# A two-layer decoder on one core: transposing the residual stream's strips on VectorE and through memory instead of on TensorE

## The chip, the cores and the metric

The kernel runs on one core of a Trainium2 chip, as one launch. The metric is device time in microseconds (us): 2370.67 us is the median of three runs (2370.56 to 2370.95). A profile shows one execution; PE is TensorE (PEld its weight loads), DVE is VectorE, ACT is ScalarE, POOL is GpSimd, SP is SyncE, and a "q" behind a name is that engine's queue of DMA issues.

## What is computed

A decoder of two layers on 256 positions with 2048 features. The first layer has stick-breaking attention, the second a dilated sliding-window attention over keys and values made once; each is followed by a gated feed-forward part with a causal convolution and by a gate on a projected per-layer input. Cut to what matters:

```python
for i in range(DEPTH):                      # DEPTH = 2
    h = rms_norm(x, attn_norm_w[i])
    if i < N_A_LAYERS:
        x = x + mixer_a(h, a_w_qkv[i], a_w_o[i])
    else:
        if i == N_A_LAYERS:
            k_blocks, v_blocks = shared_kv_blocks(x, kv_norm_w, b_w_kv, positions)
        j = i - N_A_LAYERS
        x = x + mixer_b(h, b_w_q[j], b_w_o[j], k_blocks, v_blocks, positions)
    x = x + conv_ffn(rms_norm(x, ffn_norm_w[i]), ffn_w_up[i], ffn_conv_w[i], ffn_conv_b[i], ffn_w_down[i])
    gate = jax.nn.sigmoid(rms_norm(x, ple_norm_w[i]) @ ple_w_gate[i])
    x = x + gate * (p[i].astype(x.dtype) @ ple_w_proj[i])
return rms_norm(x, final_norm_w)
```

All inputs, weights and the output are float32. The feed-forward width is 5632.

## The kernel before

**Precision.** Each float32 operand of a large product is cut in two parts, a high one of the type `F32R` and the rest, and a product is made of three matmuls: high by high, high by low, low by high. Activations are cut by `split_x` (L135 to L145; ACT writes the high part at L140, VectorE the low part at L141, and both scale by the norm's gain) or `split` (L147). Weights come from memory in tiles `raw` of four k-blocks (a k-block is 128 rows by 512 columns; 4 buffers, issued by SP at L258) and are cut in pairs of k-blocks: ACT writes `whi` (L275), VectorE `wlo` (L276), each with 4 buffers (`NWSP`).

**The stream.** The residual `x` lies in two tiles `x[0]`, `x[1]` of 128 positions by 2048 features, and is worked on in four strips of 512 features (`strip_of`). The products that read it need it the other way round, features in the partitions: `h[4*s+o]` is feature block `o` of strip `s`, 128 features by 256 positions, high part on the left and low part on the right of a 128x512 tile.

**The products.** `strip_v` (L308) makes 128 positions by 512 outputs for both halves of the positions: per k-block and half three matmuls of 512 columns (L317, L318, L319). `strip_t` (L293) makes the transposed product: four output blocks of 128, per k-block and block one matmul of 512 columns (L302) and one of 256 (L305). Both take the k-blocks in pairs, in rising order, and keep the last pair of k-blocks for the end of each output.

**The stages.** `add_strips` (L557) multiplies with `wo_a`, `wdn` or `wo_b` strip by strip, adds into `x` (L565), squares it for the norm (L212) and, where a norm follows, turns the strip: `turn` (L237) makes eight TensorE transposes of 128x128 (L244) against an identity `idf` into two PSUM banks `two`, and `split_x` reads these. `ple` (L636) does the same after the gate (L656, L659, L660), and in the first layer copies the turned strip to `xT` too (L672), for keys and values. The stage that follows reads `h` in rising order, so it can begin while the last strip is being turned. `ffn` (L573) makes the gated inputs `g` in two parts of the 11 groups of four blocks, 6 and 5 (`half`, L604), with a product with `wdn` behind each, the first of them without a norm and without turns.

**Order.** The framework's planner lays out the order of each engine's instructions ahead of time: it goes by the program's order, with pieces such as the cutting of weights moved ahead (`high_priority`, L273), and by when it expects operands and buffers by its own costs. On the chip each engine then keeps that order and waits for semaphores. Tiles named `kb` come from one ring of `NRING` = 42 buffers of 128x512 (L67, L95): `h`, `g`, `qk`, `v`, `xT` and others share them. POOL issues nothing in this kernel and SP issues the weights.

Of the kernel before, what the change touches and what calls it, by code (L numbers as in the profile page):

```python
# [10 lines left out]
F32 = mybir.dt.float32  # L11
# [3 lines left out]
AF = mybir.ActivationFunctionType  # L15
OP = mybir.AluOpType

P = 128
S = 256
# [7 lines left out]
FB = FF // P  # L27
# [36 lines left out]

RAW = 4
WARM = 9
NRING, NRAW, NWSP = 42, 4, 4  # L67
AHEAD = 200
KV_AT = (0, 6, 12, 16)
PI_PARTS = _two_pi_parts()  # L70
# [3 lines left out]
def tile_trunk(ctx, tc, head_d, xT_d, x_d, pT_d, pos_d, vec_d, cst_d, csb_d, wqkv, wo_a, wkv, wq_b, wo_b, wup, wdn, wpg, wpp, gfin_d, out_d):  # L74
    nc = tc.nc
# [2 lines left out]
    wraw = ctx.enter_context(tc.tile_pool(name="wraw", bufs=NRAW))  # L78
    wsp = ctx.enter_context(tc.tile_pool(name="wsp", bufs=NWSP))
    tmp = ctx.enter_context(tc.tile_pool(name="tmp", bufs=3))  # L80
    psum = ctx.enter_context(tc.tile_pool(name="psum", bufs=8, space=bass.MemoryType.PSUM))

    uid = [0]

    def nm(s):
        uid[0] += 1
        return f"{s}_{uid[0]}"
# [4 lines left out]
    def two_banks():  # L92
        return psum.tile([P, 2, 512], F32, tag="two", bufs=1, name=nm("two"))

    def rt(s, shape=(P, 512), dt=F32):  # L95
        return ring.tile(list(shape), dt, tag="kb", name=nm(s))

    def tt(s, shape=(P, S), dt=F32, tag=None, bufs=None):
        kw = {} if bufs is None else {"bufs": bufs}
        return tmp.tile(list(shape), dt, tag=tag or s, name=nm(s), **kw)  # L100

    f32 = lambda ap: ap.bitcast(F32)
# [3 lines left out]
    x = [cst.tile([P, D], F32, name=f"x{t}") for t in range(2)]  # L106
# [22 lines left out]
    def gain(base, j):  # L129
        return vec[:, base + j : base + j + 1]  # L130


    last = {}

    def split_x(src, j, bases):  # L135

        out = []
        for b in bases:
            h = rt("h", dt=F32R)
            last["split"] = nc.scalar.activation(h[:, :S], src, AF.Copy, scale=gain(b, j)).ins  # L140
            nc.vector.scalar_tensor_tensor(  # L141
                h[:, S:], src, gain(b, j), f32(h[:, :S]), op0=OP.mult, op1=OP.subtract
            )
            out.append(h)
        return out  # L145

# [4 lines left out]
    def strip_of(t, s):  # L151
        return x[t][:, s * 512 : (s + 1) * 512]
# [83 lines left out]

    def turn(s):  # L237

        two = two_banks()
        out = [two[:, o // 2, (o % 2) * S : (o % 2 + 1) * S] for o in range(4)]  # L240
        for o, d in enumerate(out):
            for t in (1, 0):
                c = s * 512 + o * P
                nc.tensor.transpose(d[:, t * P : (t + 1) * P], x[t][:, c : c + P], idf)  # L244
        return two, out

    def weights(W, s, n, fine=False, before=lambda k0: None, block=None, base=0, ringed=0):

# [59 lines left out]
    def strip_v(W, s, xs, base=0, tail=2, ringed=0):  # L308

        n = len(xs)  # L310
        ps = [None] * 2
        for k, t, hi, lo in (g for group in steps(weights(W, s, n, base=base, ringed=ringed), n, 2, tail) for g in group):
            if k == 0:
                ps[t] = bank("accv", "acc")
            xh = xs[k][:, t * P : (t + 1) * P]
            xl = xs[k][:, S + t * P : S + (t + 1) * P]
            nc.tensor.matmul(ps[t], xl, hi, start=k == 0, stop=False)  # L317
            nc.tensor.matmul(ps[t], xh, lo, start=False, stop=False)  # L318
            nc.tensor.matmul(ps[t], xh, hi, start=False, stop=k == n - 1)  # L319
        return ps  # L320
# [236 lines left out]
    def add_strips(W, xs, gain_of, norm, base=0):  # L557

        out = []
        for s in range(4):  # L560
            ps = strip_v(W, s, xs, base)
            if norm is not None and s == 3:
                norm.table = load_table()
            for t in range(2):
                nc.vector.tensor_tensor(strip_of(t, s), ps[t], strip_of(t, s), op=OP.add)  # L565
                if norm is not None:
                    norm.add(s, t)
            if norm is not None:
                for o, b in enumerate(turn(s)[1]):
                    out += split_x(b, 4 * s + o, [gain_of])  # L570
        return out

    def ffn(i, xs, rstd):  # L573
        cv = V_CONV + i * 4 * 2 * FB

        def conv(j, ps, y):
            col = lambda r: vec[:, cv + r * 2 * FB + j : cv + r * 2 * FB + j + 1]
            u = tt("u", tag="t", bufs=6)
            evac(ps, rstd, u)
            nc.scalar.activation(y, u, AF.Identity, scale=col(2), bias=col(3))  # L580
            nc.vector.scalar_tensor_tensor(y[:, 1:], u[:, : S - 1], col(1), y[:, 1:], op0=OP.mult, op1=OP.add)
            nc.vector.scalar_tensor_tensor(y[:, 2:], u[:, : S - 2], col(0), y[:, 2:], op0=OP.mult, op1=OP.add)

        def part(strips):
            gs = []
            for s in strips:
                ps = strip_t(wup[i], s, xs)
                gates = []
                for o in range(4):
                    y = tt("gate", bufs=4)  # L590
                    conv(4 * s + o, ps[o], y)
                    silu = nc.scalar.activation(y, y, AF.Silu).ins
                    gates.append(y)
                ps = strip_t(wup[i], FB // 4 + s, xs)
                for o in range(4):
                    y = tt("val", tag="t", bufs=6)
                    conv(FB + 4 * s + o, ps[o], y)
                    nc.vector.tensor_tensor(y, y, gates[o], op=OP.mult)
                    g = rt("g", dt=F32R)
                    split(y, g)  # L600
                    gs.append(g)
            return gs, silu

        half = (FB // 4 + 1) // 2  # L604
        gs, _ = part(range(half))
        add_strips(wdn[i], gs, None, None)
        gs, silu = part(range(half, FB // 4))
        if i == 0:
            rotary_tables(silu)
        norm = Norm()  # L610
        h = add_strips(wdn[i], gs, G_PLE + i * KB, norm, base=4 * half)
        return h, norm

# [22 lines left out]
    def ple(i, xs, ps_, rc, norm, gain_of=None):  # L636

        out, raw, gf = [], [], []
        if gain_of is None:
            for s in range(4):  # L640
                t = rt("gfin")
                nc.scalar.dma_start(
                    t, bass.AP(tensor=gfin_d.tensor, offset=gfin_d.offset + 512 * s, ap=[[0, P], [1, 512]])
                )
                gf.append(t)
        for s in range(4):
            end = gain_of is None and s == 3
            if end:
                pr = strip_v(wpp[i], s, ps_)
                gp = strip_v(wpg[i], s, xs, tail=KB, ringed=KB // 2)  # L650
            else:
                gp = strip_v(wpg[i], s, xs)
                pr = strip_v(wpp[i], s, ps_)
            for t in range(2):
                g = tt("pg", (P, 768), tag="w", bufs=2)[:, :512]
                nc.scalar.activation(g, gp[t], AF.Sigmoid, scale=rc[:, t : t + 1])  # L656
                if s == 3 and (end or t == 1):
                    norm.table = load_table()
                nc.vector.tensor_tensor(g, pr[t], g, op=OP.mult)  # L659
                nc.vector.tensor_tensor(strip_of(t, s), strip_of(t, s), g, op=OP.add)  # L660
                norm.add(s, t)
                if end:
                    finish(t, norm.half(t), gf[3])
                elif gain_of is None:
                    nc.vector.tensor_tensor(strip_of(t, s), strip_of(t, s), gf[s], op=OP.mult)
                if end and t == 0:
                    tc.keep_in_program_order(nc.scalar.preload_act_table_set("sigmoid_and_others"))
            if gain_of is not None:
                two, bs = turn(s)
                for o in range(0, 4, 2):  # L670
                    r = rt("xT")
                    nc.scalar.activation(r, two[:, o // 2], AF.Copy)  # L672
                    raw += [r[:, :S], r[:, S:]]
                    for q in range(2):
                        out += split_x(bs[o + q], 4 * s + o + q, [gain_of])
        return out, raw


    idf = cst.tile([P, P], F32, name="idf")
    warm_up()  # L680
    norm = FirstNorm()
    h = [None] * KB
# [33 lines left out]
    o = mixer_a(h, rstd, rc, first)  # L716
    for i in range(2):
        norm = Norm()
        h = add_strips(wo_a if i == 0 else wo_b, o, G_FFN + i * KB, norm)
        rstd, _ = norm.done()  # L720
        pb = p_blocks(i)
        h, norm = ffn(i, h, rstd)
        _, rc = norm.done(row=False)
        norm = Norm()
        if i == 0:
            hq, xT = ple(i, h, pb, rc, norm, G_ATTN + KB)
            rstd, rc = norm.done()
            o = mixer_b(hq, lambda js: [split_x(xT[j], j, [G_KV])[0] for j in js], rstd, rc)
# [87 lines left out]
```

## Time and profile before

| What | Value |
|---|---|
| median of three runs | 2370.67 us |
| the profiled execution's own time | 2371.05 us |
| its span, first to last instruction | 2369.3 us |
| granted TensorE clock | 0.998 |
| matmuls | 12258 |
| DMA: moved, mean rate | 442.82 MB, 187 GB/s |
| transposes of L244 | 160, 274 ns each as listed |

Busy times of engines overlap one another, so they don't add up to the span. A row of a timeline gives start, duration, engine, line, operation and, in brackets, how long the engine was idle before it and what ended that. Matmuls are pipelined: each lasts longer than the time from its start to the next one's start, and it is the starts that say what one costs.

### The profile page before, as it was taken

Reading aid. Unit: us, or ns where it says so; the run is one execution under the profiler, and the core shown is the slowest. Engines: PE = TensorE matmul, PEld = TensorE weight load, DVE = VectorE, ACT = ScalarE, POOL = GpSimd, SP = SyncE. Lnnn points to the kernel's source line nnn. Section 1 sums busy time; section 2 is a strip of 40 time slices with the busy share of each in tenths; the row PEclk is TensorE's granted clock in tenths of the full one; section 3 lists DMA queues with packets and bytes.
Section 4 is the critical chain, followed back from the end, with each engine's and each line's share of the span. In section 5 each row is a group of like instructions: output and inputs, shape, how many; then the busy total and the mean of one; then the engine's idle time right before and its main releaser. Section 6 shows DMA issues by size and latency. Waiting matters only on the chain.

```text
span 2369.3 us, 31206 instructions
## 1 busy us (share of the span) xinstructions
PE 2355.6 (99%) x12258; PEld 2004.3 (85%) x12258; DVE 1564.3 (66%) x2377; ACT 1270.5 (54%) x1826; POOL 0.2 (0%) x4
## 2 busy tenths in 40 slices
PE   9999999999999999999999999999999999999998
PEld 7888888888888888888888888888888888888886
DVE  7566555778764578765567875677776457876555
ACT  6555545656543455654565444565654345555454
POOL 0000000000000000000000000000000000000000
PEclk9999999999999999999999999999999999999999
DMA  8455455555555555555555544555555555555553
GB/s 296 174 179 182 163 178 184 194 187 187 196 187 192 190 196 184 190 194 182 184 187 194 178 147 174 183 184 190 193 183 193 195 196 184 190 192 183 193 204 116
DMA packets 64852, 442.82 MB, mean 187 GB/s; under 512 B 7200, under 2 KB 7616, under 8 KB 12736
## 3 DMA queue, kind: packets, MB, share of 16 engines
q1 hardware_dynamic: 62352, 434.93, 52.8%
q10 hardware_dynamic: 2352, 5.88, 0.8%
q8 instruction: 96, 1.57, 0.3%
q14 instruction: 52, 0.43, 0.0%
HBM read 438.69 MB, written 2.10 MB: 186 GB/s over the span
## 4 chain that ended last, share of the span: by engine, by line
PE 99%; DVE 0%; ACT 0%; DMA 0%; issue 0%; SPq 0%; DVEq 0%
PE acc L302 36%; PE acc L305 18%; PE accv L319 14%; PE accv L317 14%; PE accv L318 14%; PE two L346 2%; PE two L244 1%; PE two L420 0%; DMA raw<-in_wqkv 0%; PE keys L346 0%; PE two L421 0%; ACT whi L275 0%; DVE wlo L276 0%; ACT sq L212 0%; PE nrm L232 0%
## 5 line engine op out<-in xcount | busy, mean ns | idle before, releaser
L276 DVE TENSOR_TENSOR wlo<-raw,whi 128x1024 fp32r<-128x1024 f32 (+1 forms) x821 | 1003.9, 1223 | 722.0 <-ACT whi L275 718.6
L275 ACT ACTIVATE whi<-raw 128x1024 fp32r<-128x1024 f32 (+1 forms) x821 | 868.2, 1058 | 881.7 <-PE accv L319 426.6
L302 PE MATMUL acc<-h,whi 128*128 128x512 f32 x3712 | 1167.0, 396 | 1.9 <-DVE h L141 1.6
L305 PEld LDWEIGHTS acc<-h,wlo 128*128 128x128 f32 x3712 | 697.1, 188 | 163.3
L305 PE MATMUL acc<-h,wlo 128*128 128x256 f32 x3712 | 731.0, 278 | 0.0
L302 PEld LDWEIGHTS acc<-h,whi 128*128 128x128 f32 x3712 | 567.1, 189 | 4.6 <-DVE h L141 1.9
L319 PE MATMUL accv<-whi,g 128*128 128x512 f32 x704 | 274.7, 390 | 0.0
L318 PE MATMUL accv<-wlo,g 128*128 128x512 f32 x704 | 274.2, 390 | 0.0
L317 PE MATMUL accv<-whi,g 128*128 128x512 f32 x704 | 274.1, 389 | 0.0
L317 PE MATMUL accv<-whi,h 128*128 128x512 f32 x464 | 181.8, 392 | 0.0
L319 PE MATMUL accv<-whi,h 128*128 128x512 f32 x464 | 181.4, 391 | 0.0
L318 PE MATMUL accv<-wlo,h 128*128 128x512 f32 x464 | 181.4, 391 | 0.0
L318 PEld LDWEIGHTS accv<-wlo,g 128*128 128x128 f32 x704 | 132.2, 188 | 27.4
L319 PEld LDWEIGHTS accv<-whi,g 128*128 128x128 f32 x704 | 132.2, 188 | 27.2
L317 PEld LDWEIGHTS accv<-whi,g 128*128 128x128 f32 x704 | 132.2, 188 | 27.1
L324 ACT ACTIVATE c<-acc 128x256 f32<-128x256 f32 x232 | 86.4, 374 | 33.4 <-PE acc L305 33.4
L319 PEld LDWEIGHTS accv<-whi,h 128*128 128x128 f32 x464 | 87.2, 188 | 18.0
L317 PEld LDWEIGHTS accv<-whi,h 128*128 128x128 f32 x464 | 87.2, 188 | 17.5
L318 PEld LDWEIGHTS accv<-wlo,h 128*128 128x128 f32 x464 | 87.2, 188 | 17.4
L325 DVE TENSOR_TENSOR c<-acc,c 128x256 f32<-128x256 f32 x232 | 92.2, 418 | 0.0
L319 PE MATMUL accv<-whi,o 128*128 128x512 f32 x224 | 88.0, 393 | 0.0
L318 PE MATMUL accv<-wlo,o 128*128 128x512 f32 x224 | 87.5, 391 | 0.0
(178 smaller groups left out, 1416.9 us busy)
## 6 DMA issues: line engine op xcount, KB each, us to landing
raw<-in_wup SPq DMA_DIRECT2D x176, 1024.0 KB, 4.8
raw<-in_wdn SPq DMA_DIRECT2D x88, 1024.0 KB, 4.8
raw<-in_wqkv SPq DMA_DIRECT2D x44, 1024.0 KB, 4.9
raw<-in_wpg SPq DMA_DIRECT2D x32, 1024.0 KB, 4.9
raw<-in_wkv SPq DMA_DIRECT2D x24, 1024.0 KB, 4.8
raw<-in_wo_a SPq DMA_DIRECT2D x16, 1024.0 KB, 4.8
raw<-in_wq_b SPq DMA_DIRECT2D x12, 1024.0 KB, 4.9
raw<-in_wo_b SPq DMA_DIRECT2D x12, 1024.0 KB, 4.9
```

The source lines that it names most:

```text
L244: nc.tensor.transpose(d[:, t * P : (t + 1) * P], x[t][:, c : c + P], idf)
L275: last["high"] = nc.scalar.activation(hi[:, c], r, AF.Copy).ins
L276: nc.vector.tensor_tensor(lo[:, c], r, f32(hi[:, c]), op=OP.subtract)
L302: nc.tensor.matmul(ps[o], hi[:, c], xs[k], start=k == 0, stop=False)
L305: nc.tensor.matmul(ps[o][:, S:], lo[:, c], xs[k][:, :S], start=False, stop=k == n - 1)
L317: nc.tensor.matmul(ps[t], xl, hi, start=k == 0, stop=False)
L318: nc.tensor.matmul(ps[t], xh, lo, start=False, stop=False)
L319: nc.tensor.matmul(ps[t], xh, hi, start=False, stop=k == n - 1)
L324: last["copy"] = nc.scalar.activation(c, ps[:, S:], AF.Copy).ins
L325: last["sum"] = nc.vector.tensor_tensor(c, ps[:, :S], c, op=OP.add).ins
L346: run.append(nc.tensor.matmul(*args, skip_group_check=True, **kw).ins)
```

## The change

`turn` no longer uses TensorE. VectorE transposes each half of the strip (128 positions by 512 features) in squares of 32 by 32 into a ring tile `y`; POOL's queue writes both halves to a tile in device memory, `there`, and reads them back in four transfers, one for each 32 partitions of the result, so that every square comes to its place in the tile `turned` (128 by 8 by 4 by 32, one buffer). `split_x` and the copy to `xT` read that tile, in pieces of 32, instead of PSUM. To make room in on-chip memory the ring has 40 buffers instead of 42, and `ffn` cuts its 11 groups into 5 and 6 instead of 6 and 5.

```diff
-NRING, NRAW, NWSP = 42, 4, 4
+NRING, NRAW, NWSP = 40, 4, 4
...
+    dram = ctx.enter_context(tc.tile_pool(name="dram", bufs=2, space=bass.MemoryType.DRAM))
...
+    def like(ap, src):
+
+        return ap.rearrange("p (a r) -> p a r", r=src.shape[2]) if len(src.shape) == 3 else ap
+
     def split_x(src, j, bases):
...
             h = rt("h", dt=F32R)
-            last["split"] = nc.scalar.activation(h[:, :S], src, AF.Copy, scale=gain(b, j)).ins
-            nc.vector.scalar_tensor_tensor(
-                h[:, S:], src, gain(b, j), f32(h[:, :S]), op0=OP.mult, op1=OP.subtract
-            )
+            high, low = like(h[:, :S], src), like(h[:, S:], src)
+            last["split"] = nc.scalar.activation(high, src, AF.Copy, scale=gain(b, j)).ins
+            nc.vector.scalar_tensor_tensor(low, src, gain(b, j), f32(high), op0=OP.mult, op1=OP.subtract)
             out.append(h)
...
     def turn(s):
 
-        two = two_banks()
-        out = [two[:, o // 2, (o % 2) * S : (o % 2 + 1) * S] for o in range(4)]
-        for o, d in enumerate(out):
-            for t in (1, 0):
-                c = s * 512 + o * P
-                nc.tensor.transpose(d[:, t * P : (t + 1) * P], x[t][:, c : c + P], idf)
-        return two, out
...
+        there = dram.tile([2 * P, 512], F32, tag="turn", name=nm("there"))
+        for t in range(2):
+            y = rt("y")
+            nc.vector.transpose(
+                y.rearrange("p (b o r) -> p o b r", b=4, o=4), strip_of(t, s).rearrange("p (o b c) -> p o b c", o=4, b=4)
+            )
+            nc.gpsimd.dma_start(there[t * P : (t + 1) * P], y)
+        z = tt("turned", (P, 8, 4, 32), bufs=1)
+        back = there.rearrange("(a c) (b f) -> b c a f", c=32, b=4)
+        for b in range(4):
+            nc.gpsimd.dma_start(z[32 * b : 32 * b + 32].rearrange("p a o r -> p a (o r)"), back[b])
+        return z
...
-                for o, b in enumerate(turn(s)[1]):
-                    out += split_x(b, 4 * s + o, [gain_of])
+                z = turn(s)
+                for o in range(4):
+                    out += split_x(z[:, :, o], 4 * s + o, [gain_of])
...
-        half = (FB // 4 + 1) // 2
+        half = FB // 4 // 2
...
-                two, bs = turn(s)
+                z = turn(s)
                 for o in range(0, 4, 2):
                     r = rt("xT")
-                    nc.scalar.activation(r, two[:, o // 2], AF.Copy)
+                    nc.scalar.activation(
+                        r.rearrange("p (o a r) -> p o a r", o=2, r=32),
+                        z[:, :, o : o + 2].rearrange("p a o r -> p o a r"),
+                        AF.Copy,
+                    )
                     raw += [r[:, :S], r[:, S:]]
                     for q in range(2):
-                        out += split_x(bs[o + q], 4 * s + o + q, [gain_of])
+                        out += split_x(z[:, :, o + q], 4 * s + o + q, [gain_of])
```

## The prediction

> **What bounds the kernel now.** I read the page first, then the chain in order of time, then the timeline around one turn of a strip.
>
> ```profile
> span 2369.3 us, 31206 instructions
> ...
> PE 2355.6 (99%) x12258; PEld 2004.3 (85%) x12258; DVE 1564.3 (66%) x2377; ACT 1270.5 (54%) x1826; POOL 0.2 (0%) x4
> ...
> PE 99%; DVE 0%; ACT 0%; DMA 0%; issue 0%; SPq 0%; DVEq 0%
> ```
>
> TensorE is the bound from end to end: it is busy for 99% of the span and is 99% of the chain that ended last. So an instruction taken from it shortens the run by its own length, as long as what replaces it is in time.
>
> ```profile
> 331.39 0.87 PE two L244 x8
> 354.05 0.87 PE two L244 x8
> 376.70 0.87 PE two L244 x8
> ...
> 1049.23 0.87 PE two L244 x8
> ```
>
> The eight transposes of one `turn` (L244) stand in that chain themselves. The turns lie 22.66 us apart, and 96 matmuls (16 k, 2 halves, 3 products) lie between two of them.
>
> ```profile
> L244 PE MATMUL two<-idf,x x160: 269/273/304, 331.2 to 2262.0; 128*128 128x128 f32 x160
> ```
>
> 160 transposes are 20 turns: four strips in each of five stages (the products with `wo_a`, `wdn` twice, the first layer's `ple`, `wo_b`). How much TensorE time is one turn? Not 8 x 273 ns, since matmuls overlap; the starts tell it.
>
> ```profile
> 330.77 0.39 PE L317 MATMUL accv<-whi,o 128*128 128x512 f32 x1
> ...
> 331.00 0.39 PE L318 MATMUL accv<-wlo,o 128*128 128x512 f32 x1
> ...
> 331.23 1.04 PE L244 MATMUL two<-idf,x 128*128 128x128 f32 x8
> ...
> 332.02 0.48 PE L319 MATMUL accv<-whi,o 128*128 128x512 f32 x1
> ...
> 332.34 0.40 PE L317 MATMUL accv<-whi,o 128*128 128x512 f32 x1
> 332.57 0.39 PE L318 MATMUL accv<-wlo,o 128*128 128x512 f32 x1
> ```
>
> Matmuls of 512 columns start every 0.227 us. After 331.00 the next two would have started at 331.23 and 331.45; they started at 332.02 and 332.34. The turn cost 332.34 - 331.45 = **0.89 us** of the bound.
>
> **The change part by part.** *Removed:* 20 x 0.89 = **17.8 us** of TensorE, with no work of another engine beside it on the chain.
>
> [...]
>
> *Added on VectorE:* 40 transposes of 128x512. The trace has none; the nearest rows are elementwise work on as many elements and a shuffle of half as many.
>
> ```profile
> L565 DVE TENSOR_TENSOR x<-accv,x 128x512 f32<-128x512 f32 x48 | 30.8, 683 | 0.0
> ...
> L401 DVE STREAM_SHUFFLE sw<-qk 32x256 f32<-32x256 f32 x24 | 9.9, 434 | 0.0
> ...
> L140 ACT ACTIVATE h<-xT,vec 128x256 fp32r<-128x256 f32 x16 | 7.0, 495 | 0.0
> ...
> 309.00:400.00 91.00, 91.00 (x420) 75.58 (x419) 50.23 (x56) 45.44 (x64) 0.00 (x0) 1.00 0.54 185
> ```
>
> Between 0.68 us (L565) and 2 x 0.43 = 0.87 us (L401); I take 0.68, the row with the same 512 elements, so 1.4 us a turn. In the stage of the first four turns (last row: PE, PEld, DVE, ACT busy, clock, DMA share) VectorE works 50 of 91 us, so 5.6 us more is covered. The splits of `h` now read SBUF; the row of such a split (495 ns, against 463 from PSUM) makes 0.03 us each, on an ACT that is half idle: nothing.
>
> *Added on POOL's queue:* six DMAs a turn, two writes of 256 KB to memory and four reads of 128 KB back. POOL has done only 4 instructions, so they queue behind nothing but each other; the reads wait for both writes. They also add 1 MB to the weight stream, one weight load per turn, where a strip of 16 k has four: the DMA share goes from 0.54 to at most 0.68. A load is issued when a `raw` buffer comes free, with three more of 5.4 us full, and lands in 4.8 us:
>
> ```profile
> SPq L258 <- DVE wlo L276: 1715.8, 338, 8.1
> ...
> DMA to landing us min/median/max: 3.5/4.8/8.4
> ```
>
> Even the slowest landing, 8.4, leaves some 8 us of the 16 that lie ahead, so weights aren't late: zero.
>
> How long is the trip x to `z`? The trace has no DMA of POOL. Bounds:
>
> ```profile
> out<-x SPq DMA_DIRECT2D x4, 256.0 KB, 2.7
> ...
> pin<-in_pT ACTq DMA_DIRECT2D x2, 256.0 KB, 2.6
> ...
> x<-in_xT SPq DMA_DIRECT2D x7, 256.0 KB, 6.6
> ...
> L258 SPq DMA_DIRECT2D raw<-in_wqkv x52: 327/328/962, 1.2 to 269.2; - x52
> ```
>
> From below: issues at 0.33 us, legs at 2.7 and 2.6, so 6 x 0.33 + 5.3 = 7.3 us. From above: issues at 0.96 (the slowest of the row) and legs at 6.6, the crowded start: 5.8 + 13.2 = 19 us. I take legs from `out` and `pin` (same sizes or larger, in mid-kernel or to memory) and, as POOL's issue is unseen, the slow issue: 5.8 + 5.3 = **11.1 us**.
>
> *The new wait, in mid-strip.* ACT's split of `h` waits for `z`; behind it in ACT's order stand `whi` (L275) and the squares, behind `whi` VectorE's `wlo`, behind `wlo` TensorE. How long may ACT be held?
>
> ```profile
> 327.57 1.06 ACT L275 ACTIVATE whi<-raw 128x1024 fp32r<-128x1024 f32 x1 [1.66 <-PE accv L319]
> ...
> 330.30 1.06 ACT L275 ACTIVATE whi<-raw 128x1024 fp32r<-128x1024 f32 x1 [1.66 <-PE accv L319]
> ...
> L276 DVE TENSOR_TENSOR wlo<-raw,whi 128x1024 fp32r<-128x1024 f32 x819 | 1002.5, 1224 | 722.0 <-ACT whi L275 718.6
> ```
>
> ACT makes a `whi` each 2.72 us, when TensorE gives a buffer back; with 4 buffers three pairs (8.2 us) are then still to be used, and 1.06 + 1.22 us are needed. So ACT can stand **5.9 us** at `z` and TensorE loses nothing. The planner puts the splits where it expects `z`, not right behind the turn, so ACT stands only for the part it did not expect; 5.9 us is over half the whole trip. Cost taken: zero; without this cover, the excess over 5.9, up to 20 times.
>
> *The new wait, at the end of a stage.* The last strip's blocks h[12] to h[15] are needed soon by the next stage.
>
> ```profile
> 398.06 0.62 PE L302 MATMUL acc<-h,whi 128*128 128x512 f32 x2
> ...
> 400.32 0.62 PE L302 MATMUL acc<-h,whi 128*128 128x512 f32 x2
> ...
> 401.01 0.63 PE L302 MATMUL acc<-h,whi 128*128 128x512 f32 x2
> ...
> 397.77 1.28 DVE L565 TENSOR_TENSOR x<-accv,x 128x512 f32<-128x512 f32 x2
> ```
>
> The next stage begins at 398.06 and takes 0.695 us for each k-pair and output block, 2.78 for a pair. Six pairs come before h[12]: 16.7 us, and 0.35 for the norm's matmuls, so 415.1. x is done at 399.05; transposes 1.4, one `wlo` before them 1.2, at the end two splits on ACT and one on VectorE some 1.5: z must land within 415.1 - 399.05 - 4.1 = **12 us** of y. The trip of 11.1 fits, by 0.9. After `ple` x comes 3.4 us behind the next stage's start (1237.43 against 1234.08), not 1.0:
>
> ```profile
> 1234.08 0.62 PE L302 MATMUL acc<-h,whi 128*128 128x512 f32 x2
> ...
> 1236.75 0.68 DVE L660 TENSOR_TENSOR x<-x,pg 128x512 f32<-128x512 f32 x1
> ```
>
> There about 9.6 us are left, 1.5 us are missing. I charge **1.5 us** once. At the upper bound of 19 us it would be 4 x 7 + 9.4 = 37 us.
>
> *The rest at nothing:* 40 ring tiles for 42 are enough, since with `half` 5 the first part holds 16 + 2 + 20 = 38; in the second the last four `g` come when the 16 inputs are being given back. 5 + 6 strips of up-projection are as many matmuls as 6 + 5. `turned` has one buffer, but turns are 17 us apart or more and a trip with its splits takes some 15.
>
> **The sum:** 2371.05 (the profiled execution: span 2369.3 and 1.75 around it) - 17.8 + 1.5 = 2354.75. The median is 2370.67, 0.4 lower; I say **2355 us**.
>
> **The rivals.** *Late at the stage ends:* the trip takes 15 to 16 us, the five ends lose 3.6 on average, 18 us: **2371**. For it: the margin is 0.9 us, the raw loads' landings spread from 3.5 to 8.4. Against: a leg of 256 KB takes under 3 us in mid-kernel.
>
> [...]
>
> *The transposes' time is not given back:* something else fills it, the weight stream or ACT: **2371**. Against: in the 91 us of the stage TensorE is busy 91.00.
>
> **How the numbers follow.** Forecast 0.53 (its own range 2352 to 2360), late ends 0.22 (0.10 of it still faster, 0.08 the same, 0.04 slower), POOL held up 0.18, not given back 0.07 (0.06 the same, 0.01 slower). Faster by over 0.2% (4.7 us, about what a measurement here can tell from no change): 0.53 + 0.10 = 0.63; same 0.14; slower 0.23. Below 2352 it goes only if a turn frees more than the 0.89 us that the starts show: 0.04. To leave out no more than 0.2 above and below, the range reaches to 2390, which takes in half the upper bound's 37 us at the ends and the light cases of the held POOL; some 0.14 lies above.
>
> **What would show it.** Right: no L244 rows, strips of 16 k 21.8 us apart instead of 22.66, no TensorE idle time before `accv` in the five stages, a trip from y to the first split of `h` near 11 us. Late ends: TensorE idle before L302 or L317 some 16 us into a stage, released by a split of `h`. [...] Wrong altogether: a trip over 15 us, or ACT's splits placed ahead of the `whi` that they hold.

## The result and the profile after

The changed kernel takes **2376.84 us** in the median of 20 runs (2370.73 to 2385.79), the kernel before 2370.61 (20 runs, 2369.93 to 2371.30) on the same chip: a ratio of 1.0031, 95% interval 1.0021 to 1.0041. It is slower by 6 us where 2355 was forecast. Its runs also lie 15 us apart, where those before lie 1.4 apart. The profiled execution took 2383.19 us, 6.4 above the median, so the sums below are made for one of the longer runs.

The page of the changed kernel: the span, the busy times, the chain that ended last by engine.

```profile
span 2381.2 us, 31171 instructions
...
PE 2346.7 (99%) x12098; PEld 1993.0 (84%) x12098; DVE 1583.8 (67%) x2417; ACT 1271.4 (53%) x1826; POOL 70.0 (3%) x124
...
PE 90%; DMA 4%; DVE 2%; ACT 1%; issue 1%; POOL 1%; SPq 0%; POOLq 0%; ACTq 0%; DVEq 0%
```

TensorE was 99% of the chain and is now 90%. Transfers, VectorE, ACT and POOL have entered it: somewhere TensorE waits for the trip. The groups of the new work (busy time, mean ns of one, then the idle time before it and its releasers):

```profile
L249 DVE STREAM_TRANSPOSE y<-x 128x512 f32<-128x512 f32 x40 | 27.7, 699 | 0.0
...
L256 POOL DMA_DIRECT2D turned<-there x80 | 47.0, 594 | 103.4 <-DMA there<-y 62.0 <-ACT whi L287 40.2 <-issue 1.2
...
L252 POOL DMA_DIRECT2D there<-y x40 | 22.8, 570 | 2107.3 <-DVE y L249 2102.6 <-DVE rcol L166 4.6
...
L146 ACT ACTIVATE h<-turned,vec 128x256 fp32r<-128x256 f32 x80 | 34.7, 497 | 36.2 <-DMA turned<-there 36.2
```

VectorE's transpose takes 0.70 us, POOL's issue 0.57 to 0.59 us, a split from SBUF 0.50 us. The last row is where the time is: ACT stood 36.2 us for `turned` before its splits, at most 7.0 at once, and 12.0 us more before the copies to `xT` in `ple`. The 40.2 us of POOL put down to ACT are waits for the write too: in all 20 turns the first read is issued 0.6 to 0.8 us after the second write has landed, and the one buffer `turned` had been free for 6 us or more. The end of the `wo_a` stage in the timeline, where the worst of it is (start, duration, engine, line; in brackets the idle time before it and its releaser):

```profile
397.97 0.70 DVE L249 STREAM_TRANSPOSE y<-x 128x512 f32<-128x512 f32 x1
398.97 0.56 POOL L252 DMA_DIRECT2D there<-y  x1 [1.16 <-DVE rcol L166]
...
407.71 2.35 POOL L256 DMA_DIRECT2D turned<-there  x4 [8.19 <-DMA there<-y]
...
416.39 0.51 ACT L146 ACTIVATE h<-turned,vec 128x256 fp32r<-128x256 f32 x1 [5.51 <-DMA turned<-there]
...
417.47 1.19 PE L314 MATMUL acc<-h,whi 128*128 128x512 f32 x2 [4.67 <-DVE h L147]
```

From the end of the second transpose (398.67) to ACT's first split lie 17.7 us. POOL issued 0.3 us after the transpose; it then stood 8.2 us until the write had landed and the first read could be issued; 8.6 us lie from that issue to the last landing. TensorE then stood 4.67 us for the `h` that this makes. A second cost shows in the windows around the pauses' ends (bounds, length, busy PE, PEld, DVE, ACT, POOL with counts, granted clock, DMA share, GB/s):

```profile
417.72:421.12 3.40, 3.40 (x11) 2.77 (x11) 2.79 (x6) 2.05 (x4) 0.00 (x0) 0.51 0.18 61
1253.93:1260.75 6.82, 5.12 (x16) 4.35 (x17) 2.99 (x5) 3.71 (x8) 0.00 (x0) 0.50 0.13 26
1540.66:1547.47 6.81, 3.36 (x10) 2.92 (x11) 4.30 (x11) 2.53 (x5) 3.08 (x6) 0.50 0.69 232
2288.18:2291.58 3.40, 3.40 (x9) 2.65 (x8) 1.59 (x2) 0.79 (x1) 0.00 (x0) 0.50 0.85 286
```

**After four of the pauses the granted clock is 0.5**, for 3.4 or 6.8 us. The other stage ends in the timeline, and what half the clock does to the matmuls there:

```profile
1255.63 1.65 PE L314 MATMUL acc<-h,whi 128*128 128x512 f32 x3 [4.05 <-DVE h L147]
...
2287.40 0.50 PE L329 MATMUL accv<-whi,h 128*128 128x512 f32 x1 [1.94 <-DVE h L147]
...
2288.64 0.63 PE L330 MATMUL accv<-wlo,h 128*128 128x512 f32 x1
2289.07 0.63 PE L331 MATMUL accv<-whi,h 128*128 128x512 f32 x1
```

Matmuls that started every 0.227 us now start 0.43 us apart. The largest pause, though, is in the middle of a stage, `wo_b`, whose additions to `x` came 17.2 us apart before, little more than a trip:

```profile
1511.53 1.28 DVE L577 TENSOR_TENSOR x<-accv,x 128x512 f32<-128x512 f32 x2
...
1518.26 1.71 ACT L146 ACTIVATE h<-turned,vec 128x256 fp32r<-128x256 f32 x4 [5.18 <-DMA turned<-there]
1518.81 1.69 DVE L147 SCALAR_TENSOR_TENSOR h<-turned,vec,h 128x256 fp32r<-128x256 f32 x4 [4.47 <-ACT h L146]
1520.41 0.70 DVE L249 STREAM_TRANSPOSE y<-x 128x512 f32<-128x512 f32 x1
...
1522.71 0.70 DVE L249 STREAM_TRANSPOSE y<-x 128x512 f32<-128x512 f32 x1
...
1536.48 1.70 ACT L146 ACTIVATE h<-turned,vec 128x256 fp32r<-128x256 f32 x4 [7.00 <-DMA turned<-there]
...
1544.11 1.19 PE L236 MATMUL nrm<-diag,c 128*128 128x256 f32 x2 [6.92 <-DVE diag L234]
```

The strip's `x` was ready at 1512.8, but its transposes ran at 1520.4 and 1522.7: VectorE stood 4.47 us in the split of the strip before, behind ACT, which stood 5.18 us for the transfer. So one trip made the next one late, the next one held ACT 7.00 us, and behind the splits stood the squares and the norm, for which TensorE stood 6.92 us.

### The profile page after: what moved, and what is told of

The parts are those of the page before. It is cut to its first block, busy times and chain, and to the rows that moved or that the text cites. A ratio compares the mean times of both kernels' runs of the same rounds, so it can differ in the third digit from the quotient of the medians.

```text
span 2381.2 us, 31171 instructions
## 1 busy us (share of the span) xinstructions
PE 2346.7 (99%) x12098; PEld 1993.0 (84%) x12098; DVE 1583.8 (67%) x2417; ACT 1271.4 (53%) x1826; POOL 70.0 (3%) x124
## 4 chain that ended last, share of the span: by engine, by line
PE 90%; DMA 4%; DVE 2%; ACT 1%; issue 1%; POOL 1%; SPq 0%; POOLq 0%; ACTq 0%; DVEq 0%
PE acc L314 35%; PE acc L317 17%; PE accv L331 12%; PE accv L330 12%; PE accv L329 12%; DMA turned<-there 2%; PE two L358 2%; DMA there<-y 1%; ACT whi L287 1%; DVE wlo L288 1%; POOL turned L256 1%; ACT h L146 0%; PE two L432 0%; DMA raw<-in_wqkv 0%; DVE y L249 0%
## 5 line engine op out<-in xcount | busy, mean ns | idle before, releaser
L330 PEld LDWEIGHTS accv<-wlo,h 128*128 128x128 f32 x464 | 87.6, 189 | 17.7
```

## The experiments

In the edits, a kernel changed from the one before is named; all others start from the changed kernel. The times, with the kernel before run beside each:

| Kernel | median us (lowest to highest, runs) | before, us | ratio, 95% interval |
|---|---|---|---|
| e1_no_trip | 2352.38 (2352.14 to 2352.61, 4) | 2370.74 | 0.9923 (0.9910 to 0.9936) |
| e2_tensor_last | 2366.04 (2360.93 to 2373.84, 12) | 2370.74 | 0.9983 (0.9975 to 0.9992) |
| e3_ring_half | 2370.76 (2370.33 to 2371.20, 10, and one of these at 3942.02) | 2370.74 | 1.0000 (0.9991 to 1.0010) |
| e4_half_stream | 2357.99 (2354.34 to 2360.97, 4) | 2370.74 | 0.9946 (0.9933 to 0.9959) |
| e5_defer | 2358.30 (2356.99 to 2358.91, 5) | 2370.50 | 0.9948 (0.9935 to 0.9960) |
| e6_defer_all | 2389.86 (2387.11 to 2392.21, 5) | 2370.50 | 1.0082 (1.0068 to 1.0096) |
| e7_tensor_last_two | 2367.07 (2361.63 to 2371.20, 11) | 2370.50 | 0.9984 (0.9976 to 0.9993) |
| e8_memory_last | 2375.28 (2368.47 to 2378.06, 11) | 2370.50 | 1.0017 (1.0008 to 1.0025) |
| e9_hold_dve | 2402.13 (2400.49 to 2403.28, 4) | 2370.57 | 1.0133 (1.0116 to 1.0150) |

**Without the transfers.** VectorE transposes straight into `turned`; the placing of the squares in their partitions is left out.

```diff
-        there = dram.tile([2 * P, 512], F32, tag="turn", name=nm("there"))
+        z = tt("turned", (P, 8, 4, 32), bufs=1)
         for t in range(2):
-            y = rt("y")
             nc.vector.transpose(
-                y.rearrange("p (b o r) -> p o b r", b=4, o=4), ...
+                z[:, 4 * t : 4 * t + 4].rearrange("p b o r -> p o b r"), ...
             )
...
-        for b in range(4):
-            nc.gpsimd.dma_start(z[32 * b : 32 * b + 32].rearrange("p a o r -> p a (o r)"), back[b])
```

> The change without its transfers: VectorE transposes the squares straight into the tile `turned`, so the squares stay in the wrong partitions (the placing of the squares is left out), and everything else is as in the changed kernel. Theory A (only the trip through memory is late): TensorE waits nowhere after the start, granted clock about 0.998 as before the change, time 2371 - 17.8 = 2353 us (2351 to 2356). Rival B (the TensorE time is not given back, or VectorE's transposes, the splits from on-chip memory, the ring of 40 or the parts of 5 and 6 cost it again): 2365 us or more.

The cores' view of this kernel:

```profile
core 0: 2350.6 us, clock 0.999
```

The gain is there: 18.4 us in the medians, 18.7 in the spans, and no pause of TensorE over 0.24 us after the first 14 us. Its four runs lie 0.5 us apart, so the spread of the changed kernel belongs to the transfers as well. All of the loss comes with the trip: by its time or by the traffic that it adds, which e5 tells apart below.

**The ring and the halves alone**, in the kernel before: `NRING` 40 and `half = FB // 4 // 2`.

> The kernel before with the ring of 40 buffers and the parts of 5 and 6 groups alone. Theory A: 2370.7 us, within 1 us of before. Rival B (these two cost time in the changed kernel): 2375 us or more.

Nothing, to 0.1%. (The run of 3942 us has no profile; its cause is open.)

**The last strip of each stage by TensorE again.**

```diff
-                z = turn(s)
+                if s == 3:
+                    bs = turn_pe(s)[1]
+                else:
+                    z = turn(s)
+                    bs = [z[:, :, o] for o in range(4)]
```

> The changed kernel with the last strip of each of the five stages turned by TensorE as before, the other fifteen turns by VectorE and through memory. Theory A1 (the loss is at the stage ends): the pauses of 4.7, 0.5, 4.0 and 1.9 us go; 15 x 0.89 = 13.4 us stay won; what may be left is the pause of 6.9 us in the stage of wo_b, where ACT stood 7.0 us at the third strip: 2358 us without it, 2365 with it and its slow clock. Rival A2 (ACT held in mid-strip all over): still above 2370.

The median, 2366, is near the second of the two numbers; the profiled run, 2362.13, lies between them. In the timeline of that run:

```profile
393.10 1.71 ACT L146 ACTIVATE h<-turned,vec 128x256 fp32r<-128x256 f32 x4 [4.99 <-DMA turned<-there]
...
399.41 1.97 PE L266 MATMUL two<-idf,x 128*128 128x128 f32 x8 [3.08 <-DVE x L587]
```

The stage ends no longer wait for a trip, but a trip of the third strip (16.4 us here) holds ACT 4.99 us, VectorE behind it, the addition into `x` behind that, and TensorE stands 3.08 us before the transposes of the last strip, with 3.4 us of half clock. So the stage ends are a part of the loss, and the held ACT in mid-strip is another way in.

**Half the weight stream.** Every second load of four k-blocks is left out and the tile before is used again, so the products lack half of the weights.

```diff
-            raw = wraw.tile([P, RAW, 512], F32, tag="raw", name=nm("raw"))
+            again = not fine and w == size and (k0 // size) % 2 == 1
+            if not again:
+                raw = wraw.tile([P, RAW, 512], F32, tag="raw", name=nm("raw"))
...
-            for q in range(w) if one else (slice(0, w),):
+            for q in () if again else range(w) if one else (slice(0, w),):
```

> The changed kernel with every second weight load left out (two groups of four k-blocks use the same weights; the matmuls are as many), so the weight stream is about half: DMA share near 0.3 instead of 0.55. Theory A-stream (the weight stream makes the trip long): transfers of POOL land in some 3 us in place of 4.5 and 4.6, trips near 11 us, few pauses, about 2355 us. Rival A-POOL (the legs are long by themselves on POOL's queue, through their pieces of 512 bytes or the way POOL issues): landing times stay at 4 us or more and the time within 5 us of the changed kernel's.

The four reads of a turn, from issue to landing, in the view of the tile `turned`: first the changed kernel, then the one with half the stream.

```profile
DMA to landing us min/median/max: 2.8/4.6/8.1
```

```profile
DMA to landing us min/median/max: 2.6/2.9/6.3
```

The trip falls from 12.8 to 10.9 us in the median (8.3 to 14.1), and 18.9 of the 24.5 us that the trips cost (2376.84 less e1's 2352.38) come back. VectorE cuts as many `wlo` as before here, so it isn't VectorE that makes the trip long; it is the weights in flight. What gets shorter is the reads: from the first read's issue to the last landing it is 4.7 us instead of 6.7 in the median. The second write still takes 5.2; in 13 of the 20 turns of both kernels SP issues a load 0.9 us ahead of it. Sorted by how long a weight load was in flight beside it, the 40 writes of the changed kernel fall in two heaps: 14 with under 2.5 us beside one land in 2.5 us in the median, 26 with more in 5.2 (up to 8.0). In this kernel it is 19 at 2.5 and 21 at 5.2. (A slow transfer meets more of a load in any case, and 12 of the 14 are the first write of their turn. For the reads the cause is shown by halving the stream; for the writes it rests on this sorting.) What is left in the profiled run, 2360.97, is a pause of 3.32 us at the end of `ple`, behind a trip of 14.1.

**The last strip by TensorE, and ACT's and VectorE's splits of the other strips queued behind the squares of the next strip**, by when the trip is over.

```diff
-                for o in range(4):
-                    out += split_x(z[:, :, o], 4 * s + o, [gain_of])
+                if late:
+                    with tc.issue_after(last["square"]):
+                        for j, b in late:
+                            out += split_x(b, j, [gain_of])
...
+                late = [(4 * s + o, b) for o, b in enumerate(bs)]
+        for j, b in late:
+            out += split_x(b, j, [gain_of])
```

> The last strip of each stage turned by TensorE, and the splits of the other strips queued on ACT behind the squares of the strip that follows, so that ACT meets a `turned` that landed long ago. Theory C (what was left in e2_tensor_last is ACT, and VectorE behind it, standing at a split before the trip is over): no pauses of TensorE after the start, clock 0.998, 2371 - 15 x 0.89 = 2357.5 us and a spread of runs as small as before the change (1 to 2 us). Rival D (the runs' spread comes from the added traffic itself, weights that come late): still 2361 to 2374.

The waits for `turned` (us in all, times, longest) in the changed kernel, then in this one:

```profile
ACT h L146 <- DMA turned<-there: 36.2, 15, 7.0
```

```profile
ACT h L146 <- DMA turned<-there: 7.1, 2, 4.5
```

2358.30, within 1 us of what was expected, and runs 2 us apart: **faster than both kernels**, by 12 us than the one before. The fifteen trips are as long as before, 12.6 us in the median (11.6 to 16.1), and no pause over 0.26 us is left after the first 14 us: neither a trip of up to 16.1 us nor its traffic costs anything here, where nothing due stands behind it. Over e1 it has 5.9 us, of which the five turns that TensorE makes are 5 x 0.89 = 4.5.

**The same deferral with all strips through memory.**

> All twenty turns through memory, with the first three strips' splits of each stage queued behind the next strip's squares. Theory C: only the stage ends are left: four or five pauses of TensorE of 0.5 to 5 us, each with 3.4 or 6.8 us of half clock behind the longer ones, so 2353 + about 11 + about 7: 2368 to 2374, and the 6.9 us pause in the stage of wo_b gone. Rival: no better than the changed kernel, 2377 or more.

The theory's range is missed by 16 us, and the rival's holds. In the timeline, at the end of `wo_a`:

```profile
402.77 0.70 DVE L249 STREAM_TRANSPOSE y<-x 128x512 f32<-128x512 f32 x1
...
416.87 0.51 ACT L146 ACTIVATE h<-turned,vec 128x256 fp32r<-128x256 f32 x1 [3.62 <-DMA turned<-there]
...
417.95 1.65 PE L324 MATMUL acc<-h,whi 128*128 128x512 f32 x3 [2.88 <-DVE h L147]
```

The deferred splits of the third strip now stand ahead of the last strip's transposes, so the last trip begins at 403.5 (398.7 in the changed kernel). All five stages end with a pause, of 2.6 to 5.4 us, and 3.4 to 6.8 us of half clock behind each. What helps in mid-strip harms at the end, where nothing may stand before the trip.

**The last two strips by TensorE** (`s >= 2`), without deferral, and **only the last strips through memory** (`s < 3` by TensorE): the two ways in, each alone.

> The last two strips of each stage turned by TensorE, the first two through memory, no splits deferred. Theory C: a held ACT in the first strips costs TensorE little, as nothing near a stage's end waits: 2371 - 10 x 0.89 = 2362 us, at most 2365. Rival (any trip in mid-strip costs by itself): 2366 or more, like e2_tensor_last.

> Only the last strip of each stage goes through memory, the other fifteen are turned by TensorE. Theory A1 (stage ends): 5 x 0.89 = 4.5 us won, pauses of some 11 us in all at the ends and 5 to 10 us of half clock's loss: 2377 to 2387. Rival A2 (the loss in the changed kernel comes from mid-strip holds): 2367 to 2370.

e7 lies above the theory's range in the median, and in the rival's. Its profiled run (2363.60) has no pause over 0.44 us after the first 15 us; the others are up to 7.6 us longer, and since its stage ends have no trip, what remains is ACT held in mid-strip (5.5 us at most in that run); that this is what costs in the longer runs, and at which places, no profile shows. e8 lies between its two ranges. It saves 5 x 0.89 = 4.5 us of transposes and is still 4.8 slower than before, so its five trips at the ends lose some 9 us in the median; its profiled run, one of the quickest at 2370.82, shows two of them, pauses of 1.58 and 1.44 us, and no half clock. So the ends alone lose 9 of the 24.5 us. Taking them away (e2) won 10.8 and put 4.5 us of transposes back, 15 of the 24.5: the difference may be what a late strip in the middle adds to the end behind it, which no run takes apart.

**What a held VectorE costs by itself**, without any transfer of POOL's: the kernel before, with a long sum on VectorE behind six strips of the products with `wdn` that no norm follows.

```diff
+    def hold(t, n):
+
+        d = tt("held", (P, 32), bufs=1)
+        nc.vector.reduce_sum(d[:, :n], t.unsqueeze(1).to_broadcast([P, n, 512]), axis=mybir.AxisListType.X)
...
+            if norm is None and s < 3:
+                HOLD["n"] = HOLD.get("n", -1) + 1
+                hold(strip_of(1, s), (8, 12, 16, 20, 24, 32)[HOLD["n"]])
```

> The kernel before, with one long VectorE instruction put into each of six strips of the first products with wdn, where nothing is turned (a sum over 8, 12, 16, 20, 24 and 32 readings of 512 elements, about 4.3, 6.4, 8.6, 10.7, 12.9 and 17.1 us; its result is not used). VectorE, and wlo behind it, stands still for that long. Theory E1 (cover of about 5.9 us, then each pause of TensorE of some 2 us or more is followed by 3.4 or 6.8 us of half clock): pauses of about 0, 0.5, 2.7, 4.8, 7 and 11.2 us, sum 26, and 4 stretches of half clock that cost 1.7 to 3.4 us each: 2403 to 2411 us. Rival E2 (the slow clock in the changed kernel has another cause, such as the transfers): the same pauses at full clock, 2395 to 2398 us. Rival E3 (no cover): pauses as long as the holds, 2425 us or more.

The last four sums and the pauses behind them in its timeline:

```profile
766.38 8.69 DVE L562 TENSOR_REDUCE held<-x 128x16 f32<-128x8192 f32 x1
...
776.25 0.50 PE L318 MATMUL accv<-wlo,g 128*128 128x512 f32 x1 [2.13 <-DVE wlo L276]
...
1831.45 10.82 DVE L562 TENSOR_REDUCE held<-x 128x20 f32<-128x10240 f32 x1
...
1843.46 0.79 PE L318 MATMUL accv<-wlo,g 128*128 128x512 f32 x1 [4.27 <-DVE wlo L276]
...
1870.10 12.95 DVE L562 TENSOR_REDUCE held<-x 128x24 f32<-128x12288 f32 x1
...
1884.24 0.80 PE L318 MATMUL accv<-wlo,g 128*128 128x512 f32 x1 [6.40 <-DVE wlo L276]
...
1910.94 17.22 DVE L562 TENSOR_REDUCE held<-x 128x32 f32<-128x16384 f32 x1
...
1929.35 0.80 PE L318 MATMUL accv<-wlo,g 128*128 128x512 f32 x1 [10.66 <-DVE wlo L276]
```

The median, 2402.13, is 0.9 us under the range of theory E1 and above that of E2. Hold less pause is 6.56, 6.55, 6.55 and 6.56 us: the cover that the cut weights give a held VectorE (a held ACT wasn't tried so). The two shorter holds, 4.42 and 6.55, make no pause. The time lost at each place against the kernel before, matmul by matmul, is more than the pause: 2.5 us for the pause of 2.13, 6.0 for 4.27, 8.2 for 6.40, 13.7 for 10.66. With the three longer ones the rest is nearly all the clock, in the windows that hold the pauses:

```profile
766.40:776.20 9.80, 7.72 (x35) 6.05 (x33) 9.80 (x3) 3.39 (x4) 0.00 (x0) 1.00 0.01 4
1843.15:1846.55 3.40, 3.09 (x7) 2.48 (x8) 3.40 (x4) 0.00 (x0) 0.00 (x0) 0.50 0.57 176
1880.69:1887.51 6.82, 3.27 (x8) 2.59 (x9) 6.82 (x5) 0.00 (x0) 0.00 (x0) 0.50 0.31 102
1921.65:1935.30 13.65, 5.95 (x14) 4.70 (x15) 11.24 (x6) 1.06 (x1) 0.00 (x0) 0.50 0.36 136
```

No half clock with the pause of 2.13; 3.4, 6.8 and 13.65 us of it with the three longer ones, part of it inside the pause and part behind it. So the clock fell to 0.5 also with pauses of 4.27, 6.40 and 10.66 us that VectorE alone had made, without a transfer of POOL's.

## Why the prediction was wrong

- **The transposes taken from TensorE, 17.8 us: right.** e1 gains 18.4.
- **VectorE's part, the splits, the ring, the halves at nothing: right.** 0.699 us where 0.68 was taken, 0.497 where 0.495; e1 and e3 show no cost.
- **The trip of 11.1 us: this step failed.** It is 9.6 to 17.6 us over the 20 turns, 12.8 in the median: 0.3 to the second write's issue, 5.2 until it has landed, 0.6 to the first read's issue, 6.7 until the last read has landed (three more issues of 0.59 lie in it). The issue was taken too dear (0.96, measured 0.57 to 0.59), the legs too cheap: 2.7 and 2.6 from `out` and `pin`, rows of four and two transfers, against 4.5 for a write and 4.6 for a read in the medians. Those rows tell of transfers that hardly meet a weight load: none is in flight beside `out`, 0.4 and 0.5 us of one beside the two of `pin`. In e1, where POOL issues nothing, the same `pin` meets 4.0 and 4.3 us of one and already differs (transfers, KB each, median us to landing):

```profile
pin<-in_pT ACTq DMA_DIRECT2D x2, 256.0 KB, 4.5
```

  The 14 writes of POOL's that hardly met a weight load landed in 2.5 us, about the price taken from the two rows; the other 26, two of three, took 5.2, up to 8.0. Two trips, 15.3 and 17.6, pass the 15 us that the prediction named as a sign of being wrong.
- **The budget of 12 us at a stage's end, 9.6 behind `ple`: right.** Trips of 17.6, 12.7, 14.1 and 14.1 us at four ends exceed it by 5.6, 0.7, 4.5 and 2.1; the pauses are 4.67, 0.52, 4.05 and 1.94. The rival "late at the stage ends" named this mechanism, and its 18 us is what the four ends lose in the profiled run (17.8 in the sum below, 11.2 of it as pauses); what it had at nothing is the middle of the stages, 12.5 in that run.
- **Mid-strip at zero, with a cover of 5.9: nothing speaks against the cover, but what was counted behind the held ACT is wrong; this step failed too.** In e7 ACT stood 5.5 us without a pause of TensorE, and the 6.55 of e9, for a held VectorE, fits. The placing of the splits didn't spare ACT: in 18 of the 20 turns it came to `turned` before the last read had landed. Behind it only `wlo` was followed to TensorE; the squares were named, but not the norm that needs them. The next strip's addition, transposes, squares and norm stand there too, and in `wo_b` a strip is hardly longer than a trip. That is the pause of 6.92 us. The same in small in `ple`, some 2 us. e5, which takes the splits out of that place, loses none of it.
- **The clock behind a pause: not in the prediction.** TensorE worked 3.40 + 5.12 + 3.36 + 3.40 = 15.3 us in the four windows at half clock, which is 7.6 us lost. The four stretches are 3.4 or 6.8 us long (3.4, 6.8 and 13.65 in e9). A pause of 1.94 us was followed by one, a pause of 2.13 in e9 by none.
- **POOL held up, the rival at 0.18: no run shows an issue of POOL's held by VectorE.** Issues are steady at 0.57 and 0.59 us in the medians (0.71 at most) with VectorE 67% busy, and e4 shortens the trip with VectorE's `wlo` as many as before. The slower result came by another way.

The sum, for the profiled execution, matmul by matmul against e1, which has the same matmuls: 6.6 us are lost at the end of `wo_a`, 0.9 at the end of the first `wdn`, 2.6 in `ple`, 6.3 at its end, 9.9 in `wo_b`, 4.0 at the end of the second `wdn`, 30.3 in all. Of it 20.1 us are TensorE idle, 7.6 the clock; 2.6 are left that no row names. 2350.6 and 30.3 make 2380.9, where the span is 2381.2. In the median run the loss is 24.5, by trips that happen to be shorter.

## What to carry to other kernels

A transfer's price must be taken from rows that meet the same traffic as it will, and at the slow end of their spread where its margin is 0.9 us. Before work is moved from the bound to a path with a long latency, list all that stands behind each waiting instruction on its engine, and keep what is due at once (here the last strip of a stage) on the short path: e5 keeps two thirds of the gain so. A pause of the bound cost more than its length where the clock fell: 13.7 us for one of 10.66 in e9.

## What the runs showed of the hardware

- In the changed kernel a write of 256 KB to memory landed in 2.5 us in the median with under 2.5 us of a 1 MB weight load beside it (14 writes), in 5.2 with more (26), at a mean DMA share of about half. A read of 128 KB back landed in 4.6 us there, and in 2.9 with half the weight stream (e4).
- The granted clock fell to 0.5 in four stretches of the changed kernel, of 3.4, 6.8, 6.8 and 3.4 us, from 417.67, 1253.93, 1540.65 and 2288.17 on; in e9 in stretches of 3.4, 6.8 and 13.65, part of them inside the pause. The length of the pause alone doesn't decide at the small end: 1.94 us at 2285.5 brought 3.4 us of it; 1.44 and 1.58 in e8, 1.56 in e6 and 2.13 in e9 brought none. What sets the 1.94 apart from the 2.13 was not shown.
- POOL issued a write of 256 KB in 0.57 us and a read of 128 KB in 0.59, in the medians, and VectorE transposed 128x512 float32 in squares of 32 in 0.70 us, where an elementwise addition of that size took 0.68 before.
